# A hybrid streaming layer on one core: the sink column is written after the score product, VectorE makes every low half of a weight, and the second phase is laid out with another table of costs

## The chip, the cores and the metric

The kernel runs on one core of one Trainium2 chip. The metric is the device time of one execution in microseconds (us): 1554.15 us before the change, the median of three runs (1549.72 to 1560.18). Engines are named as the profile names them: PE is TensorE (PEld its weight load), DVE is VectorE, ACT is ScalarE, POOL is GpSimd, and SP is SyncE, which only issues transfers.

## The reference, cut to what matters

One layer of a streaming encoder, for 2048 prompt frames and 32 sample frames, 1024 wide, in fp32:

```python
h = rmsnorm(x, ln_g)
q, k, v, gate_a, b_gate, c_gate, u_in, gate_c, merge_a, merge_c = split(h @ w_in)
q, k = rope(rmsnorm(q)), rope(rmsnorm(k))             # 8 q heads, 2 kv heads, 64 wide
s = q @ k.T                                           # own chunk of 64 and the two before it
m = maximum(max(s), sink)
p = exp(s - m) / (sum(exp(s - m)) + exp(sink - m))    # sink: one learned number per head
y_a = (p @ v * silu(gate_a)) @ w_attn_out
y_c = (b_gate * conv3(c_gate * u_in) * silu(gate_c)) @ w_conv_out
r = x + (sigmoid(merge_a) * y_a + sigmoid(merge_c) * y_c) @ w_o
out = r + sigmoid(r @ w_ple_gate) * (p_in @ w_ple_proj)
```

The sink takes part in the softmax like one more key whose score is a constant.

## The kernel before

**Precision.** A product in fp32 is made of three products of split operands: each operand x is kept as a high half (a copy in the type fp32r) and a low half (x minus the high half), and hi·hi, hi·lo and lo·hi are added in PSUM. So every operand costs a copy on ACT (`..._h`) and a subtraction (`..._l`), and every 128x512 block of weights a cast on ACT and a subtraction, both written into a tile `w`.

**Two phases.** The first phase (to about 850 us) makes h @ w_in by a Strassen scheme and leaves its parts in DRAM. The second phase, the one the change touches, does everything else: yB (the convolution branch times its output weights), pp (p_in @ w_ple_proj), 17 attention tiles of 128 frames (16 of the prompt, with two chunks of 64 frames each, and one of the 32 sample frames), yA (attention times its weights), and two large products per half of the frames, UO (with w_o) and UPG (with w_ple_gate), again by a Strassen scheme; these are the `b` of the profile, and their results `c`. Their inputs `xb` are split too, after sums and differences on DVE (`tk`, `c`).

**Attention.** A chunk's chain, in `sink_attention` (L1230), is: ACT copies the sink into one column of the PSUM tile `S` (L1235); PE makes the scores into the columns beside it; DVE takes the negative maximum of scores and sink (`nm`, L1246); ACT makes the exponentials with their sum (`E`, L1253); DVE takes the reciprocal (`se`); ACT scales (`P`); PE transposes (`PT`); ACT and DVE split the result (`pth`, `ptl`); PE multiplies by the values (`O`); DVE multiplies by the gate (`at`). Since the copy of L1235 and the products write one tile, the product stands behind the copy. Ahead of the chain, a tile's queries and keys are transposed (`pq`, `pkv`), normed and rotated on DVE (`tt`, `ss`, `kn`, `qr`, `kr`) with two operations on POOL (`ab`, and a power of -0.5 on `ss`), transposed back (`pk`, `pqt`) and split (`KH`, `KL`, `qs`).

**What sets the order.** In the second phase no scheduler moves anything: a small planner inside the kernel, run while the program is built, writes each engine's instructions in the order in which its own clock reaches them. Each operation goes through `Engine` (L115), which asks `cost` (L101) for a duration, adds it to that engine's `busy` time and notes when the result is there; a step that needs a result is entered into a list with that time plus 0.15 (`SEM`). PE's clock `now` moves by PE's costs alone; `due` (L173) takes the next step whose time has come and whose buffers are free. So attention steps, evictions and splits are laid between PE's products according to these costs. The attention tiles are started at fixed amounts of PE's work, two chunks of a tile 5 us apart (`GAP`, L1992).

**Weights.** `split_w` (L1884) makes a block's halves: the cast on ACT and then the subtraction, on POOL for blocks ahead of `last_split` (L1895: the first block of the second half's large products), 88 of them, and on DVE for those after it. Five tiles `w` are in use at a time.

Since all of this goes through `Engine`, nearly every instruction of the second phase has line L136 in the profile, and the names of the tiles tell them apart.

Of the kernel before, what the change touches and what calls it, by code (L numbers as in the profile page):

```python
# [7 lines left out]
F32 = mybir.dt.float32  # L8
F32R = mybir.dt.float32r
AF = mybir.ActivationFunctionType  # L10
ALU = mybir.AluOpType
# [31 lines left out]
def tile_hybrid_stream_step(ctx: ExitStack, tc: tile.TileContext, x, xT, pT, wu, consts, rope, ckT, cv_dup,  # L43
                            ck_raw, cv_raw, yT, kpo, vpo, cpo, kso, vso, cso):
    nc = tc.nc
    add, sub, mul = ALU.add, ALU.subtract, ALU.mult
# [10 lines left out]
    def bank(name):  # L57
        return psp.tile([P, 512], F32, tag="ps", name=name)
# [28 lines left out]
    now, fin, seq, events = [0.0], [0.0], [0], []  # L87
    busy = {"V": 0.0, "S": 0.0, "G": 0.0, "Y": 0.0}
# [6 lines left out]
    def size(ap):  # L95
        n = 1
        for d in ap.shape[1:]:
            n *= d
        return n

    def cost(key, op, kw):  # L101
        if op == "dma_start":
            return 0.9 if kw.get("accum_op") is not None else 0.57 if key == "G" else 0.42
        n = size(kw["out"])
        if key == "T":
            return max(0.109, 0.00044 * n + 0.0064)
        if key == "S":
            return 0.2 + 0.00082 * n + (0.13 if kw.get("accum_out") is not None else 0.0)
        if key == "G":
            return 2.03 if kw.get("op") == ALU.pow else 0.35 + 0.0021 * n  # L110
        if op == "tensor_reduce":
            return 0.08 + 0.0012 * size(kw["in_"])
        return 0.3 if n <= 16 else 0.13 + 0.0011 * n

    class Engine:  # L115
        def __init__(self, key, engine):
# [2 lines left out]
        def __getattr__(self, op):  # L119
            f = getattr(self.engine, op)  # L120

            def call(**kw):
                us = cost(self.key, op, kw)
                if self.key == "T":
                    now[0] += us
                    end = now[0]
                else:
                    busy[self.key] = end = max(busy[self.key], now[0]) + us
                if op == "dma_start":
                    if wire[0] is None:  # L130
                        end += 6.6 if kw.get("accum_op") is not None else 5.2
                    else:
                        o = kw["out"]
                        wire[0] = end = max(end + 1.7, wire[0]) + o.shape[0] * size(o) * 4 / 390e3
                fin[0] = max(fin[0], end)
                return f(**kw)  # L136
            return call

    eV, eS, eG, eT, eY = [Engine(*x) for x in (("V", nc.vector), ("S", nc.scalar), ("G", nc.gpsimd), ("T", nc.tensor),
                                           ("Y", nc.sync))]  # L140
# [5 lines left out]
    def free(tag, n=1):  # L146
        live[tag] -= n
        assert live[tag] >= 0, tag
# [40 lines left out]
    def restart():  # L189
        assert not events  # L190
        now[0], banks[0], wire[0] = 0.0, 0, None
        for x in (busy, live):
            for k in x:
                x[k] = 0
        live["k"] = 24
# [25 lines left out]
    G = len(groups)  # L221
# [78 lines left out]
    def tile_of(gs, q):  # L300
        return "AB GF DE C".split().index(next(x for x in "AB GF DE C".split() if q in x)) if len(gs) == 2 else q == "C"

    worder = []
    for s in steps:
        for s_ in s:
            key = ("s", *s_) if len(s_) == 3 else ("l", *s_[1:3], tile_of(s_[1], s_[3]))
            if key not in worder:
                worder.append(key)
    for kind, b, n, *p in plan:
        key = {"B": (kind, b, n, *p), "yB": ("q", 0, UY + n, 1), "pp": ("pp", b, n // 2),  # L310
               "yA": ("q", b, UY + n, 0)}[kind]
        key = ("pp", 2, n // 2) if kind == "pp" else key
# [181 lines left out]
    def norm(v, k, rb, q):  # L494
        nc.vector.scalar_tensor_tensor(out=v, in0=v, scalar=lng_sb[:, k:k + 1], in1=rb[:, :q], op0=mul, op1=mul)
# [8 lines left out]
    B, T = {}, {}  # L504
# [718 lines left out]
    nc.gpsimd.memset(sq, EPS)  # L1223

    restart()
    order[0] = lambda e: e[:3]

    def sink_attention(name, ng, lhs, krhs, cn, e_out, norm, keys, sk, done, last, lag):  # L1230
        GG = 2 * ng
        SS = []
        for kv in range(2):
            s = bank(f"S_{name}_{kv}").rearrange("p (g c) -> p g c", g=2)
            eS.copy(out=s[:, :ng, cn:cn + 1], in_=sk[:, kv * ng:(kv + 1) * ng].unsqueeze(2))  # L1235
            kh, kl = krhs(kv)
            for j in range(ng):
                eT.matmul(out=s[:, j, :cn], lhsT=lhs(kv, j), rhs=kh, start=True, stop=False)
                eT.matmul(out=s[:, j, :cn], lhsT=lhs(kv, j), rhs=kl, start=False, stop=True)
            SS.append(s)  # L1240
        if last:
            free("qs")
        yield {}
        nmax = sm.tile([P, 4], F32, tag="nmax", name=f"nm_{name}")
        for kv in range(2):
            eV.tensor_reduce(out=nmax[:, kv * ng:(kv + 1) * ng], in_=SS[kv][:, :ng, :cn + 1],  # L1246
                            axis=AX.X, op=ALU.max, negate=True)
        yield {}
        se = sm.tile([P, 4], F32, tag="se", name=f"se_{name}")
        for kv in range(2):  # L1250
            for j in range(ng):
                g = kv * ng + j
                eS.activation(out=e_out(kv, j), in_=SS[kv][:, j, :cn + 1], func=AF.Exp, bias=nmax[:, g:g + 1],  # L1253
                              accum_out=se[:, g:g + 1])
            yield None
            yield None
        yield {}
        free("ps", 2)
        eV.reciprocal(out=se[:, :GG], in_=se[:, :GG])
        yield {}  # L1260
        for kv in range(2):
            for j in range(ng):
                g = kv * ng + j
                for src, dst in norm(kv, j):
                    eS.activation(out=dst, in_=src, func=AF.Copy, scale=se[:, g:g + 1])
            if kv == 0:
                yield None
        fin[0] += lag
        yield {"ps": 2, "ph": 1}
        w = ng * P  # L1270
        pts, parts = [], []
        for q0 in range(0, len(keys), 512 // w):
            qs = keys[q0:q0 + 512 // w]
            pp = bank(f"PT_{name}_{q0}")
            for i, (ins, kp_, vh, vl) in enumerate(qs):
                for j, src in enumerate(ins):
                    eT.transpose(out=pp[:kp_, i * w + j * P:i * w + (j + 1) * P], in_=src, identity=ident)
            cols = 256 if q0 else 512
            ph = sm.tile([P, cols], F32R, tag=f"pth{cols}", name=f"pth_{name}_{q0}", bufs=2)
            pl = sm.tile([P, cols], F32R, tag=f"ptl{cols}", name=f"ptl_{name}_{q0}", bufs=2)  # L1280
            i = 0
            while i < len(qs):
                e = i
                while e < len(qs) and qs[e][1] == qs[i][1]:
                    e += 1
                n = qs[i][1]
                parts.append((ph[:n, i * w:e * w], pl[:n, i * w:e * w], pp[:n, i * w:e * w]))
                i = e
            pts += [(ph[:n, i * w:(i + 1) * w], pl[:n, i * w:(i + 1) * w], vh[:n], vl[:n])
                    for i, (_, n, vh, vl) in enumerate(qs)]  # L1290
        yield {}
        free("P")
        for h, _, src in parts:
            eS.copy(out=h, in_=src)
        yield {}
        for x, (h, lo, src) in enumerate(parts):
            if x:
                yield None
            eV.tensor_tensor(out=lo, in0=src, in1=h.bitcast(F32), op=sub)
        yield {"ps": -1}  # L1300
        O = bank(f"O_{name}")
        for i, (ph, pl, vh, vl) in enumerate(pts):
            eT.matmul(out=O[:, :w], lhsT=vh, rhs=ph, start=(i == 0), stop=False)
            eT.matmul(out=O[:, :w], lhsT=vl, rhs=ph, start=False, stop=False)
            eT.matmul(out=O[:, :w], lhsT=vh, rhs=pl, start=False, stop=(i == len(pts) - 1))
        yield {}
        free("ph")
        done(O)
        yield {}
        free("ps")  # L1310
        if last:
            last()
# [571 lines left out]
    def split_w(i):  # L1884
        w = wp.tile([P, 2, 4, P], F32R, tag="w", name=f"w{i}")
        W2[i] = h, lo = w[:, 0], w[:, 1]
        src = raw_of.pop(i)
        eS.copy(out=h, in_=src)
        yield {}
        (eG if i < last_split else eV).tensor_tensor(out=lo, in0=src, in1=h.bitcast(F32), op=sub)  # L1890
        yield {}
        w_ready[i] = now[0]
        room["wf"] += 1

    last_split = next(i for i, key in enumerate(worder) if key[:2] == ("B", 1))  # L1895
    x_at, load_at = [0], [0]
    LEAD, LOOK = 2, 11

# [89 lines left out]
    T, t = {}, 0.0  # L1988
# [116 lines left out]
```

## Time and profile before

| what | value |
|---|---|
| median of three runs | 1554.15 us (1549.72 to 1560.18) |
| the profiled execution | 1554.51 us, its span 1552.7 us |
| mean granted clock of PE | 0.990 |
| busy, whole span: PE, DVE, ACT, POOL | 1504.6, 1219.8, 816.9, 491.6 us |
| 830 to 1086 us (A): PE, DVE, ACT, POOL | 241.69, 184.32, 156.63, 81.07 of 256 us |
| 1086 to 1330 us (B): PE, DVE, ACT, POOL | 221.83, 217.39, 159.71, 134.55 of 244 us |
| 1330 to 1540 us (C): PE, DVE, ACT, POOL | 210.00, 158.99, 96.56, 42.85 of 210 us |

The span runs from the first to the last instruction; the execution's own time is 1.8 us longer. A is the stretch of yB, pp, yA of the first quarter and about half of the attention; B holds the first half's large products and the rest of the attention; C is the second half's large products. A row of grouped instructions gives the count, the busy time and the mean duration of one, then the idle time of the engine ahead of them and what ended it. A row of waits gives who waited for whom, the total in us, the number of times and the longest. Engines work in order, and a duration in the profile includes the time in which an operation that has been started is held up.

### The profile page before, as it was taken

Reading aid. Unit: us, or ns where it says so; the run is one execution under the profiler, and the core shown is the slowest. Engines: PE = TensorE matmul, PEld = TensorE weight load, DVE = VectorE, ACT = ScalarE, POOL = GpSimd, SP = SyncE. Lnnn points to the kernel's source line nnn. Section 1 sums busy time; section 2 is a strip of 40 time slices with the busy share of each in tenths; the row PEclk is TensorE's granted clock in tenths of the full one; section 3 lists DMA queues with packets and bytes.
Section 4 is the critical chain, followed back from the end, with each engine's and each line's share of the span. In section 5 each row is a group of like instructions: output and inputs, shape, how many; then the busy total and the mean of one; then the engine's idle time right before and its main releaser. Section 6 shows DMA issues by size and latency. Waiting matters only on the chain. (4 is left out here: it accounts for less than half of the span.)

```text
span 1552.7 us, 28012 instructions
## 1 busy us (share of the span) xinstructions
PE 1504.6 (97%) x9553; PEld 1358.6 (87%) x9553; DVE 1219.8 (79%) x2242; ACT 816.9 (53%) x1933; POOL 491.6 (32%) x622
## 2 busy tenths in 40 slices
PE   9999999999999999999999999999988997999998
PEld 7878888888899999999999899887877886999998
DVE  7887878875689777899757678857799899569777
ACT  8453353344467544344556356775755676444453
POOL 2133322232212332344212222236647455410201
PEclk9999999999999999999999999999999999999999
DMA  9489886898778845344647766567847659995959
GB/s 336 156 295 341 312 301 211 270 348 274 248 255 276 284 160 159 118 135 133 196 162 251 246 221 202 185 184 222 195 122 197 155 170 270 256 266 143 256 146 279
DMA packets 199230, 346.88 MB, mean 223 GB/s; under 512 B 23728, under 2 KB 57072, under 8 KB 199088
## 3 DMA queue, kind: packets, MB, share of 16 engines
q1 hardware_dynamic: 157008, 239.42, 48.2%
q0 software_dynamic: 32432, 87.85, 19.8%
q10 hardware_dynamic: 9648, 17.83, 3.1%
q8 instruction: 75, 1.23, 0.3%
q14 instruction: 67, 0.55, 0.1%
HBM read 227.66 MB, written 117.46 MB: 222 GB/s over the span
## 5 line engine op out<-in xcount | busy, mean ns | idle before, releaser
L136 PE MATMUL b<-xb_h,w 128*128 128x264 f32 (+1 forms) x1344 | 314.2, 325 | 0.0
L136 PEld LDWEIGHTS b<-xb_h,w 128*128 128x128 f32 x1344 | 225.5, 190 | 19.0
L591 PE MATMUL a<-x_l,w 128*128 128x264 f32 (+1 forms) x744 | 228.1, 320 | 0.0
L589 PE MATMUL a<-x_h,w 128*128 128x264 f32 (+1 forms) x744 | 227.2, 320 | 0.1
L136 PE MATMUL b<-xb_l,w 128*128 128x264 f32 (+1 forms) x672 | 218.1, 325 | 0.0
L594 PE MATMUL a<-x_h,w 128*128 128x264 f32 (+1 forms) x744 | 201.5, 320 | 0.0
L207 ACT CAST w<-wr 128x512 fp32r<-128x512 f32 (+1 forms) x180 | 110.1, 618 | 105.2 <-PE c L594 34.5
L208 DVE TENSOR_TENSOR w<-wr,w 128x512 fp32r<-128x512 f32 (+1 forms) x180 | 136.6, 769 | 34.4 <-ACT w L207 34.0
L136 POOL TENSOR_TENSOR w<-wr,w 128x512 fp32r<-128x512 f32 x88 | 127.0, 1495 | 110.5 <-ACT w L136 96.1
L136 ACT CAST w<-wr 128x512 fp32r<-128x512 f32 x168 | 102.5, 620 | 106.1 <-PE b L136 31.5
L589 PEld LDWEIGHTS a<-x_h,w 128*128 128x128 f32 x744 | 139.9, 188 | 10.8 <-DVE s L795 0.3
L591 PEld LDWEIGHTS a<-x_l,w 128*128 128x128 f32 x744 | 139.7, 188 | 10.7
L136 PEld LDWEIGHTS b<-xb_l,w 128*128 128x128 f32 x672 | 127.8, 190 | 9.5
L594 PEld LDWEIGHTS a<-x_h,w 128*128 128x128 f32 x744 | 125.0, 188 | 10.5
L727 PE MATMUL la<-x_h,w 128*128 128x264 f32 x516 | 111.7, 285 | 1.2 <-ACT w L207 1.2
L589 PE MATMUL c<-x_h,w 128*128 128x512 f32 (+1 forms) x336 | 110.6, 340 | 0.0
L591 PE MATMUL c<-x_l,w 128*128 128x512 f32 (+1 forms) x336 | 110.7, 339 | 0.0
L207 ACT CAST w<-a 128x512 fp32r<-128x512 f32 x82 | 49.7, 621 | 98.2 <-DVE a L338 31.8
L594 PE MATMUL c<-x_h,w 128*128 128x512 f32 (+1 forms) x336 | 100.4, 340 | 0.0
L788 DVE SCALAR_TENSOR_TENSOR u<-u,c 128x264 f32<-128x264 f32 (+1 forms) x125 | 59.4, 507 | 44.8 <-ACT u L783 29.8
L136 PE MATMUL yB<-ycs_h,w 128*128 128x264 f32 (+1 forms) x384 | 91.0, 326 | 0.0
L136 PE MATMUL yA<-ac_h,w 128*128 128x264 f32 (+1 forms) x384 | 90.5, 325 | 0.0
(436 smaller groups left out, 3949.0 us busy)
## 6 DMA issues: line engine op xcount, KB each, us to landing
wr<-in_wu SPq DMA_DIRECT2D x177, 256.0 KB, 4.0
a<-in_wu SPq DMA_DIRECT2D x116, 256.0 KB, 5.2
wr<-ws SPq DMA_DIRECT2D x74, 256.0 KB, 3.5
wr<-qs SPq DMA_DIRECT2D x64, 256.0 KB, 4.1
ws<-a POOLq DMA_DIRECT2D x63, 256.0 KB, 4.0
qs<-a POOLq DMA_DIRECT2D x24, 256.0 KB, 5.7
z_s<-s2n POOLq DMA_DIRECT2D x21, 264.0 KB, 4.2
s<-z_s SPq DMA_DIRECT2D x21, 264.0 KB, 5.0
```

What stands on the lines that cost most here:

```text
L136: return f(**kw)
L207: nc.scalar.copy(out=hi, in_=src)
L208: nc.vector.tensor_tensor(out=lo, in0=src, in1=hi.bitcast(F32), op=sub)
L589: nc.tensor.matmul(out=ps[:, :cn], lhsT=w[:, 0, k], rhs=x[0][:, c0:c0 + cn], start=first and k == 0, stop=False, skip_group_check=True)
L591: nc.tensor.matmul(out=ps[:, :cn], lhsT=w[:, 0, k], rhs=x[1][:, c0:c0 + cn], start=False, stop=False, skip_group_check=True)
L594: nc.tensor.matmul(out=ps[:, :cn], lhsT=w[:, 1, k], rhs=x[0][:, c0:c0 + cn], start=False, stop=k == 3, skip_group_check=True)
L727: nc.tensor.matmul(out=ps[:, :m], lhsT=w[:, a, k], rhs=r[:, cols], start=q in "ABG" and j == 0 and e == 0, stop=j == 1 and e == 2, skip_gr ...
L788: nc.vector.scalar_tensor_tensor(out=t[:, c0:c0 + cn], in0=t[:, c0:c0 + cn], scalar=-1.0, in1=ps[:, :cn], op0=mul, op1=sub)
```

## The change

1. In `sink_attention`, the copy of the sink into its column comes after both products, as a step of its own; the maximum follows it as before.
2. In `split_w`, all subtractions go to DVE: the 88 that POOL made are now DVE's.
3. From the start of the second phase the planner uses a second table of costs, `cost_queue`. It charges an operation of DVE 0.085 less and one of ACT 0.1 less than `cost` did (a reduction 0.07 less, a very small operation on DVE 0.09 in place of 0.3), PE nearly the same, an accumulating transfer on POOL 0.6 in place of 0.9. The result is noted as there 0.08 (DVE), 0.1 (ACT) or 0.25 (POOL) after the engine is free (`LATE`), and each operation of POOL that isn't a transfer also charges DVE 0.35 of its cost (`BESIDE`).

The reads and writes, the amount of arithmetic, the transfers and their sizes are the same.

```diff
+    LATE = {"V": 0.0, "S": 0.0, "G": 0.0, "Y": 0.0}
+    BESIDE = [0.0]
+
     def cost(key, op, kw):
+        if LATE["V"]:
+            return cost_queue(key, op, kw)
         if op == "dma_start":
             return 0.9 if kw.get("accum_op") is not None else 0.57 if key == "G" else 0.42
         n = size(kw["out"])
...
+    def cost_queue(key, op, kw):
+        if op == "dma_start":
+            return 0.6 if key == "G" else 0.42
+        n = size(kw["out"])
+        if key == "T":
+            return max(0.1085, 0.000446 * n + 0.0028)
+        if key == "S":
+            return 0.1 + 0.00082 * n + (0.13 if kw.get("accum_out") is not None else 0.0)
+        if key == "G":
+            return 2.03 if kw.get("op") == ALU.pow else 0.35 + 0.0021 * n
+        if op == "tensor_reduce":
+            return 0.01 + 0.0012 * size(kw["in_"])
+        return 0.09 if n <= 16 else 0.045 + 0.0011 * n
+
     class Engine:
...
-                    busy[self.key] = end = max(busy[self.key], now[0]) + us
+                    busy[self.key] = max(busy[self.key], now[0]) + us
+                    end = busy[self.key] + LATE[self.key]
+                    if self.key == "G" and op != "dma_start":
+                        busy["V"] = max(busy["V"], now[0]) + BESIDE[0] * us
...
     restart()
+    LATE.update(V=0.08, S=0.1, G=0.25)
+    BESIDE[0] = 0.35
     order[0] = lambda e: e[:3]
...
             s = bank(f"S_{name}_{kv}").rearrange("p (g c) -> p g c", g=2)
-            eS.copy(out=s[:, :ng, cn:cn + 1], in_=sk[:, kv * ng:(kv + 1) * ng].unsqueeze(2))
...
         if last:
             free("qs")
+        yield {}
+        for kv in range(2):
+            eS.copy(out=SS[kv][:, :ng, cn:cn + 1], in_=sk[:, kv * ng:(kv + 1) * ng].unsqueeze(2))
         yield {}
         nmax = sm.tile([P, 4], F32, tag="nmax", name=f"nm_{name}")
...
-        (eG if i < last_split else eV).tensor_tensor(out=lo, in0=src, in1=h.bitcast(F32), op=sub)
+        eV.tensor_tensor(out=lo, in0=src, in1=h.bitcast(F32), op=sub)
```

The first phase's instructions stand as before. In the second, three places show what the change moves. The first is ACT around the sink copies of chunk 20 (`S_20_0`, `S_20_1`), in stretch B; `xb050_6_3_h` and its like are high halves of inputs of a large product, `c12_...` an eviction of one, `sq` and `VH` belong to the next attention tile. Before:

```order
L136 ACTIVATE sq_10098<-pkv2_3_13621 128x2x64
L136 CAST w396_13651<-wr396_13304 128x512
L136 CAST VH_10094<-pkv2_3_13621 64x64 x4
L136 COPY c12_050_3_1_13668<-b050_3_1_0_13603 128x512
L136 ACTIVATE xb050_6_3_h_13675<-tk0_3_12617 128x512
L136 ACTIVATE xb050_7_0_h_13683<-tk1_0_13005 128x512
L136 COPY S_20_0_13691<-cst_69 128x2
L136 COPY S_20_1_13697<-cst_69 128x2
```

and with the change:

```order
L158 ACTIVATE xb050_6_2_h_13594<-tk0_2_12635 128x512
L158 CAST w395_13606<-wr395_13270 128x512
L158 COPY c12_050_2_1_13623<-b050_2_1_0_13589 128x512
L158 COPY S_20_0_13629<-cst_69 128x2
L158 COPY S_20_1_13634<-cst_69 128x2
L158 CAST w396_13654<-wr396_13343 128x512
```

The copies now stand ahead of the next tile's `sq` and `VH` and of the weight block w396, which they stood behind; the product itself stands 24 matmuls earlier in PE's order than it did.

The second is DVE around the maxima of the same chunk (`nm_20`). Before:

```order
L136 TENSOR_TENSOR tt2_3_13636<-pkv2_3_13621,ab2_3_13624 128x256
L136 TENSOR_REDUCE ss2_3_13656<-sq_10098 128x10
L136 TENSOR_TENSOR c11_050_3_2_12917<-c11_050_3_2_12917,b050_3_1_0_13603 128x512
L136 SCALAR_TENSOR_TENSOR xb050_6_3_l_13676<-tk0_3_12617,xb050_6_3_h_13675 128x512
L136 SCALAR_TENSOR_TENSOR xb050_7_0_l_13684<-tk1_0_13005,xb050_7_0_h_13683 128x512
L136 TENSOR_REDUCE nm_20_13712<-S_20_0_13691 128x2
```

and with the change:

```order
L158 TENSOR_TENSOR w395_13606<-wr395_13270,w395_13606 128x512
L158 TENSOR_TENSOR tk1_7_13456<-tk1_7_13456,tc1_7_13458 128x512
L158 TENSOR_TENSOR c11_050_2_2_12899<-c11_050_2_2_12899,b050_2_1_0_13589 128x512
L158 TENSOR_TENSOR tk1_3_13382<-tk1_7_13456,tk1_3_13382 128x512
L158 SCALAR_TENSOR_TENSOR tk0_3_12693<-tk0_3_12693,tk1_3_13382 128x512
L158 TENSOR_REDUCE nm_20_13665<-S_20_0_13629 128x2
L158 TENSOR_REDUCE nm_20_13665<-S_20_1_13634 128x2
L158 TENSOR_TENSOR w396_13654<-wr396_13343,w396_13654 128x512
```

The subtractions of w395 and w396 stand in DVE's queue around the maxima, which come before the next tile's `tt` and `ss`.

The third is POOL near the end of the same product's evictions, in the middle of B (`c..<-in_xT` are accumulating transfers, `ss` is the power, `KH` and `KL` copies of keys). Before:

```order
L136 TENSOR_TENSOR ss3_0_14301<-ss3_0_14301,nhalf_70 128x10
L136 DMA c12_050_2_1_13626<-in_xT 128x512
L136 TENSOR_TENSOR w410_14357<-wr410_13934,w410_14357 128x512
L136 TENSOR_TENSOR w411_14359<-wr411_13992,w411_14359 128x512
L136 TENSOR_TENSOR w412_14383<-wr412_14091,w412_14383 128x512
L136 DMA c12_050_3_1_13668<-in_xT 128x512
L136 TENSOR_TENSOR w413_14415<-wr413_14109,w413_14415 128x512
L136 COPY KH_10092<-KH_10092 128x2x128
L136 COPY KL_10093<-KL_10093 128x2x128
```

and with the change:

```order
L158 TENSOR_TENSOR ss3_0_14356<-ss3_0_14356,nhalf_70 128x10
L158 DMA c12_050_2_1_13623<-in_xT 128x512
L158 DMA c12_050_3_1_13688<-in_xT 128x512
L158 DMA c21_050_0_7_13900<-in_xT 128x512
L158 DMA c21_050_1_7_13929<-in_xT 128x512
L158 COPY KH_10092<-KH_10092 128x2x128
L158 COPY KL_10093<-KL_10093 128x2x128
```

POOL keeps its transfers, powers and copies, and none of the four subtractions.

More of the change, by code (lines that the diff above doesn't have):

```diff
@@ L1893, in split_w @@
         room["wf"] += 1
-    last_split = next(i for i, key in enumerate(worder) if key[:2] == ("B", 1))
     x_at, load_at = [0], [0]
```

## The prediction

> **What bounds the kernel now.** I read the page's engine line first, then busy time by stretch, then PE's waits, then PE's clock, and last DVE's and POOL's groups in the stretch that loses most.
>
> ```profile
> PE 1504.6 (97%) x9553; PEld 1358.6 (87%) x9553; DVE 1219.8 (79%) x2242; ACT 816.9 (53%) x1933; POOL 491.6 (32%) x622
> ```
> ```profile
> core 0: us, PE busy (x) PEld busy (x) DVE busy (x) ACT busy (x) POOL busy (x), PEclk, DMA share, GB/s
> 830.00:1086.00 256.00, 241.69 (x1638) 221.78 (x1637) 184.32 (x389) 156.63 (x487) 81.07 (x72) 0.98 0.70 219
> 1086.00:1330.00 244.00, 221.83 (x1122) 184.49 (x1121) 217.39 (x357) 159.71 (x454) 134.55 (x113) 0.96 0.72 188
> 1330.00:1540.00 210.00, 210.00 (x1718) 209.53 (x1717) 158.99 (x299) 96.56 (x182) 42.85 (x47) 1.00 0.83 220
> ```
>
> PE bounds the whole, and no amount of PE's work is changed. So the change can only win what PE loses: idle time and lowered clock. In C (1330 to 1540) PE is never idle, and the 13 us after it are the last results' way out: nothing to win. A loses 14.3 us, B 22.2 us, and only these have a clock below 1. B is also where DVE is fullest, 217.4 of 244 us. PE's waits in A, then in B:
>
> ```profile
> PE S L136 <- ACT S L136: 5.1, 5, 2.5
> PE S L136 <- DVE kn L136: 3.8, 1, 3.8
> PE pq L136 <- DMA zq<-z_q: 3.0, 1, 3.0
> ```
> ```profile
> PE S L136 <- ACT S L136: 13.3, 6, 5.8
> PE O L136 <- DVE ptl L136: 8.7, 3, 5.1
> ```
>
> Nearly everything is a score product S that waits for the sink copy on ACT. (The wait put down to kn is one too: it is the 4.0 us in which ACT was busy 3.95, two rows below.) After such gaps the clock is halved. Of the windows here, 1007.9, 1076.4 and 1130.2 are gaps, the others the halved stretches behind these and behind two gaps at O:
>
> ```profile
> 1007.90:1011.90 4.00, 0.27 (x3) 0.06 (x1) 3.71 (x11) 3.95 (x16) 2.52 (x2) 1.00 0.94 271
> 1011.90:1015.30 3.40, 3.37 (x15) 3.37 (x16) 3.20 (x7) 0.88 (x4) 0.00 (x0) 0.50 0.16 48
> 1076.40:1079.20 2.80, 0.34 (x4) 0.13 (x2) 2.77 (x9) 2.80 (x11) 2.80 (x5) 1.00 0.74 233
> 1080.10:1083.50 3.40, 3.40 (x14) 3.01 (x14) 1.31 (x4) 1.29 (x3) 0.81 (x2) 0.51 0.66 205
> 1134.80:1141.60 6.80, 5.14 (x16) 4.47 (x17) 5.39 (x11) 5.07 (x14) 4.51 (x4) 0.50 0.46 93
> 1203.00:1209.80 6.80, 6.03 (x18) 5.06 (x19) 6.73 (x13) 2.77 (x8) 2.46 (x2) 0.50 0.56 148
> 1319.10:1325.90 6.80, 6.09 (x22) 5.51 (x23) 3.79 (x9) 4.01 (x14) 3.02 (x3) 0.50 0.96 233
> ```
>
> Half of the busy time in these is lost: 1.7 + 1.7 = 3.4 us in A, 2.6 + 3.0 + 3.0 = 8.6 us in B. So a gap of 3 us costs nearly 5.
>
> Why is ACT late with its copies in B? Because it waits for DVE, and DVE for POOL:
>
> ```profile
> 1308.54 5.78 DVE L136 SCALAR_TENSOR_TENSOR ac_l<-acf,ac_h 128x528 fp32r<-128x528 f32 x1
> ```
> ```profile
> 1308.42 5.32 POOL L136 TENSOR_TENSOR w<-wr,w 128x512 fp32r<-128x512 f32 x4
> ```
>
> One DVE operation takes 5.78 us, exactly as long as four subtractions of weights on POOL run. It isn't one accident. The groups of DVE in B, and the two after them in the stretch 1340 to 1540, where POOL has almost no such work:
>
> ```profile
> L136 DVE TENSOR_TENSOR xb_l<-c,xb_h 128x512 fp32r<-128x512 f32 x28 | 29.1, 1054 | 2.4 <-ACT xb_h L136 2.2
> L136 DVE TENSOR_TENSOR c<-c,b 128x512 f32<-128x512 f32 x35 | 23.6, 677 | 7.1 <-PE b L136 5.6 <-ACT c L136 1.4
> L136 DVE SCALAR_TENSOR_TENSOR xb_l<-tk,xb_h 128x512 fp32r<-128x512 f32 x20 | 18.4, 940 | 0.1
> L136 DVE SCALAR_TENSOR_TENSOR c<-c,c 128x512 f32<-128x512 f32 x12 | 12.5, 1045 | 0.1
> L136 DVE SCALAR_TENSOR_TENSOR c<-c,pp 128x512 f32<-128x512 f32 x13 | 11.0, 853 | 0.1
> L136 DVE SCALAR_TENSOR_TENSOR ac_l<-acf,ac_h 128x528 fp32r<-128x528 f32 x4 | 7.9, 1970 | 0.0
> L136 DVE TENSOR_TENSOR kn<-tt 128x64 f32<-128x64 f32 x12 | 6.9, 572 | 0.0
> L136 DVE TENSOR_TENSOR VL<-pkv,VH 64x64 fp32r<-64x64 f32 x24 | 5.3, 220 | 0.3
> ```
> ```profile
> L136 DVE TENSOR_TENSOR w<-wr,w 128x512 fp32r<-128x512 f32 x64 | 43.7, 686 | 9.7 <-ACT w L136 9.3 <-DMA pp<-z_pp 0.2
> L136 DVE TENSOR_TENSOR xb_l<-c,xb_h 128x528 fp32r<-128x528 f32 x28 | 19.0, 701 | 1.8 <-ACT xb_h L136 1.7
> ```
>
> Operations that read PSUM (c<-c,b, VL) keep 677 and 220 ns; those that read two tensors from SBUF are held up. Over 680 ns (701 for ac_l, 220 for kn) that is 28 x 0.374 + 20 x 0.26 + 12 x 0.365 + 13 x 0.173 + 4 x 1.27 + 12 x 0.352 = 31.6 us in B. The smaller groups add some more.
>
> **The change part by part.** *The sink copy behind the product.* It takes away the waits at S: 5.1 + 3.8 = 8.9 us in A, 13.3 us in B. The copy itself stays on ACT and now lies in the chain between product and maximum:
>
> ```profile
> 1078.91 0.28 ACT L136 COPY S<-cst 128x2 f32<-128x2 f32 x2
> ```
>
> So each of the 32 prompt chunks' chains becomes at least 0.28 us longer, and where ACT's queue is late the maximum is late. That costs nothing as long as PE has other products between S and PT, as it has: PE never waits at PT in A or B, and ACT waits for PE there instead:
>
> ```profile
> ACT pth L136 <- PE PT L136: 15.7, 6, 8.7
> ```
>
> If that cover were gone, the price would be 32 x 0.28 = 9 us or more. The copy can now hold up ACT until PE has made the product; queued behind it at chunk 20 is the cast of w396, then DVE's half of w396. Late next after S are PT (on P) and O (on ptl).
>
> *The subtractions.* POOL loses and DVE gains 25 in A, 58 in B and 5 after it:
>
> ```profile
> L136 POOL TENSOR_TENSOR w<-wr,w 128x512 fp32r<-128x512 f32 x58 | 84.3, 1524 | 55.0 <-ACT w L136 52.4 <-DMA pp<-z_pp 1.6 <-issue 0.7
> L136 POOL TENSOR_TENSOR ss<-ss,nhalf 128x10 f32<-128x10 f32 x6 | 13.0, 2169 | 6.6 <-DVE ss L136 6.6
> L136 POOL TENSOR_TENSOR ab<-cs,cst 128x256 f32<-128x256 f32 x6 | 6.6, 1094 | 0.0
> ```
> ```profile
> L136 POOL TENSOR_TENSOR w<-wr,w 128x512 fp32r<-128x512 f32 x25 | 34.7, 1405 | 55.3 <-ACT w L136 43.5 <-ACT S L136 11.8
> ```
>
> A duration of 0.68 isn't what one takes of DVE's time, since starts are closer:
>
> ```profile
> 1126.42 0.68 DVE L136 TENSOR_TENSOR tk<-tk,tc 128x512 f32<-128x512 f32 x1
> 1127.02 0.67 DVE L136 TENSOR_TENSOR c<-c,b 128x512 f32<-128x512 f32 x1
> ```
>
> 0.60 us from start to start. So DVE gains 58 x 0.60 = 34.8 us in B. What it gets back is the hold-up by these 58: they are 84.3 of the 103.9 us of POOL's arithmetic above, 81%, so 0.81 x 31.6 = 25.6 us. DVE in B: 217.4 - 25.6 + 34.8 = 226.6 us. In A: 184.3 + 25 x 0.60 = 199.3 of 256 us, well covered by PE. So in B DVE isn't relieved; its work is even a little more. What changes is its kind: lumps of 2 to 6 us that the planner knew nothing of become operations of 0.6 us that stand in its table. And the floor of B is no longer PE's 221.8 less its 8.6 of half clock, 213 us, but DVE's 227, if DVE were never idle.
>
> *The order.* Costs nothing by itself. It takes 0.085 to 0.1 us per operation out of the plan, which was a margin by accident (0.69 planned against 0.60 from start to start) and is now given to the 88 subtractions and to POOL's hold-ups.
>
> **The sum**, against the profiled execution's 1554.5 us (0.4 above the median, so no correction). A: 8.9 us of waits and 3.4 of clock go; the wait for zq (3.0 us, a transfer) stays; with longer chains and less margin I take 3 back at PT and O: gain 9.3. B: between 227 us (DVE never idle) and 244 (nothing gained). DVE now idles 26.6 us in B, mostly waiting for PE's own products (5.6 in the row of c<-c,b), and these come sooner when PE doesn't wait. I take the end near the full DVE, 231: gain 13. C: 0. 1554.5 - 9.3 - 13 = 1532 us.
>
> On the clock, the Trainium skill's "TensorE: Matmul & The Clock Gate" (What's actually happening) says that PE falls to half its clock after at least one idle window of about 3.4 us. By that the gap of 2.8 us at 1076.4 wouldn't have led to the half clock behind it, and A's gain would be 1.7 less, 1534 us in all; the trace shows the half clock, so I keep it.
>
> **Rivals.**
> *DVE isn't the floor (PE runs through).* Weights and inputs of the large products are prepared far ahead, so DVE's backlog may run over into C, where it is busy 159 of 210 us. Then B falls to 213 and A gives all: 1554.5 - 12.3 - 31 = 1511 us. For it: no wait of PE for w or xb in the rows. Against: attention's DVE operations stand in the same queue. Chance 0.12.
> *The waits move (no change).* S no longer waits, but PT and O do: ACT's and DVE's backlog is still there, the plan lost its margin and each chain got the copy. An ACT chain of ten operations from S to P loses 10 x 0.1, gets back two handovers of 0.1 and pays the copy's 0.28: about 1 us per chunk. If 25 of 33 chunks stall by it: 1532 + 25 = 1557 us. For it: the O waits, already there at 8.7. Against: none at PT. Chance 0.14.
> *DVE saturates (slower).* If the hold-up doesn't go with POOL's subtractions (the powers and transfers that remain hold DVE as long), DVE in B needs 217.4 + 34.8 = 252 us, and with the 26.6 idle it has now 279: 35 more, 1554.5 - 9.3 + 35 = 1580 us. It decides as soon as less than 8 us of the 31.6 go, with DVE never idle. Against: the 5.78 us beside four POOL subtractions, and 686 ns per w where POOL is quiet. Chance 0.07.
> *DVE holds POOL.* The 58 subtractions on DVE read two tensors from SBUF and may hold POOL's powers just as POOL's held DVE: 7 in B by up to 0.68, 5 us in the chain ss, kr, pk; 1537 us. Chance 0.05. The Trainium skill's "SBUF — State Buffer" (SBUF: two separate sides) says so: whichever of the two starts first has the shared ports for its whole instruction, and the other is blocked; the 5.78 us agree for POOL first, no row here shows the other way alone.
>
> **How the numbers follow.** The forecast, B near DVE's floor, has 0.62; its own range is 1518 to 1544, from no give-back in A and B at 220 (the smaller held-up groups counted too) to B at 240 and a gain of 6 in A. The range of 8 in 10 reaches to the first two rivals: 1511 to 1553. A measurement of this kernel can tell about 1% from no change, 15.5 us. Faster by more (below 1539): 0.62 x 0.9 + 0.12 + 0.05 x 0.6 = 0.71, and some of the moved waits: 0.74. Slower by more: 0.07, and 0.02 of the moved waits: 0.09. Within 1%: 0.17.
>
> **What would show it.** Right: no row of PE at S waiting for ACT; POOL's w gone, DVE's w x88 more; xb_l<-c back near 700 ns in B; DVE's busy time in B at 215 to 230 of a shorter stretch; PE's remaining waits at O and PT below 10 us; C unchanged; fewer half-clock stretches, with the one behind zq left. Wrong: xb_l still near 1 us; PE waiting at PT or O for 20 us; PE waiting for w or xb.

## The result and the profile after

The changed kernel takes 1530.11 us (median of four runs, 1526.45 to 1533.35); the kernel before took 1552.41 us on the same chip (median of four, 1549.72 to 1560.18). The ratio is 0.9848, with a 95% interval of 0.9804 to 0.9892, all of it below 1: faster, by about 22 us or 1.5%. The profiled execution took 1533.35 us, its span 1531.6.

The page's engine line, and the busy time by stretch; A, B and C now end at 1076, 1312 and 1525 us:

```profile
PE 1500.7 (98%) x9553; PEld 1355.8 (89%) x9553; DVE 1227.2 (80%) x2330; ACT 818.2 (53%) x1933; POOL 370.5 (24%) x534
```
```profile
830.00:1076.00 246.00, 239.72 (x1654) 221.44 (x1653) 191.66 (x416) 159.50 (x493) 48.20 (x47) 0.99 0.72 226
1076.00:1312.00 236.00, 222.82 (x1141) 184.94 (x1140) 216.84 (x419) 159.88 (x443) 55.52 (x57) 0.96 0.74 199
1312.00:1525.00 213.00, 213.00 (x1752) 213.00 (x1751) 165.71 (x310) 98.25 (x192) 34.55 (x40) 1.00 0.83 228
```

PE's losses in A shrink from 14.3 to 6.3 us and in B from 22.2 to 13.2 us; C has none, as before. DVE makes 62 operations more in B than before and is busy for as long, 216.84 us against 217.39. POOL is busy for 55.5 us there in place of 134.6. PE's waits in A and then in B:

```profile
PE pq L158 <- DMA zq<-z_q: 3.2, 1, 3.2
PE lc L749 <- DVE o L765: 1.3, 1, 1.3
PE pp L158 <- ACT E L158: 1.0, 1, 1.0
PE PT L158 <- ACT P L158: 0.7, 1, 0.7
```
```profile
PE b L158 <- DVE c L158: 4.5, 3, 3.3
PE PT_s L158 <- ACT Ps L158: 3.2, 1, 3.2
PE b L158 <- ACT xb_h L158: 2.8, 1, 2.8
PE pq L158 <- ACT E L158: 1.4, 1, 1.4
PE b L158 <- DVE xb_l L158: 0.8, 2, 0.5
PE PT L158 <- ACT P L158: 0.5, 1, 0.5
```

No score product waits for a copy, and no O for ptl. The copy waits for the product now, which costs ACT time that it has; in B:

```profile
ACT S L158 <- PE S L158: 14.3, 17, 5.2
```

What is left in B are a few waits of the large products: for an eviction that frees a bank (c), for inputs (xb), and one for the sample frames' scaled exponentials (Ps). Three of these waits (for xb_h, Ps and c) and the one for zq each end in a halved clock. In the windows over these four places, the window and its length come first, then the busy time of PE, PEld, DVE, ACT and POOL, and the clock is the third figure from the right:

```profile
883.50:886.90 3.40, 3.40 (x18) 3.38 (x17) 0.17 (x1) 1.43 (x4) 0.73 (x1) 0.50 1.04 397
1125.80:1129.20 3.40, 3.40 (x13) 2.92 (x13) 2.93 (x9) 3.40 (x12) 0.17 (x1) 0.51 0.54 77
1207.80:1214.60 6.80, 5.63 (x17) 4.68 (x18) 6.62 (x17) 3.41 (x11) 1.98 (x1) 0.50 0.25 69
1272.60:1279.40 6.80, 5.63 (x13) 4.46 (x14) 6.80 (x13) 1.83 (x3) 0.47 (x1) 0.50 1.07 315
```

DVE's groups in B that were held up before:

```profile
L158 DVE TENSOR_TENSOR w<-wr,w 128x512 fp32r<-128x512 f32 x60 | 43.2, 723 | 0.5 <-ACT w L158 0.2
...
L158 DVE TENSOR_TENSOR xb_l<-c,xb_h 128x512 fp32r<-128x512 f32 x28 | 18.6, 682 | 3.0 <-ACT xb_h L158 2.9
...
L158 DVE SCALAR_TENSOR_TENSOR xb_l<-tk,xb_h 128x512 fp32r<-128x512 f32 x20 | 13.8, 715 | 0.6 <-ACT xb_h L158 0.5
L158 DVE SCALAR_TENSOR_TENSOR c<-c,pp 128x512 f32<-128x512 f32 x15 | 10.2, 684 | 0.1
...
L158 DVE SCALAR_TENSOR_TENSOR c<-c,c 128x512 f32<-128x512 f32 x12 | 8.1, 685 | 0.2
...
L158 DVE SCALAR_TENSOR_TENSOR ac_l<-acf,ac_h 128x528 fp32r<-128x528 f32 x4 | 2.6, 696 | 0.0
```

Operations that took 853 to 1970 ns take 682 to 715. The 60 new ones in B have 43.2 us of busy time, and at the prediction's 0.60 us from start to start they take 36 of DVE's. Since DVE's total in B stands, the hold-up that went is about as large (an estimate from these rows). So DVE got 60 operations more in B and no more load there; in the whole execution it is busy for 1227.2 us in place of 1219.8.

### The profile page after: what moved, and what is told of

The parts are those of the page before. It is cut to its first block, busy times and chain, and to the rows that moved or that the text cites. A ratio compares the mean times of both kernels' runs of the same rounds, so it can differ in the third digit from the quotient of the medians.

```text
span 1531.6 us, 27944 instructions
## 1 busy us (share of the span) xinstructions
PE 1500.7 (98%) x9553; PEld 1355.8 (89%) x9553; DVE 1227.2 (80%) x2330; ACT 818.2 (53%) x1933; POOL 370.5 (24%) x534
## 4 chain that ended last, share of the span: by engine, by line
PE 38%; DVE 7%; ACT 3%; DMA 2%; issue 2%; SPq 0%; ACTq 0%; DVEq 0%
PE b L158 17%; PE yB L158 5%; PE yA L158 5%; PE O L158 2%; PE S L158 2%; DVE c L158 1%; PE la L749 1%; PE pp L158 1%; PE a L611 1%; PE a L613 1%; PE a L616 1%; PE PT L158 1%; DVE w L158 1%; DVE xb_l L158 1%; DVE tk L158 1%
## 5 line engine op out<-in xcount | busy, mean ns | idle before, releaser
L158 PE MATMUL b<-xb_l,w 128*128 128x264 f32 (+1 forms) x672 | 218.4, 325 | 0.8 <-DVE xb_l L158 0.8
L158 DVE TENSOR_TENSOR w<-wr,w 128x512 fp32r<-128x512 f32 x168 | 117.8, 706 | 14.1 <-ACT w L158 13.4
L805 ACT COPY u<-a 128x264 f32<-128x264 f32 (+1 forms) x114 | 47.4, 437 | 80.7 <-PE a L616 80.7
```

Of the source, the lines that this page charges most:

```text
L805: nc.scalar.copy(out=t[:, c0:c0 + cn], in_=ps[:, :cn])
```

## The experiments

The change has three edits, so the first question is which of them carries the gain: each alone, and the change without each. Then the hold-up is measured by itself, then the parts of the table. All stretches below are cut at the same products of PE (the starts of the 5,001st, the 6,652nd and the last of the 9,540 in its order, without the first 13 of the execution's 9,553), from the trace's start times: A is then 257.8 us before and 245.9 after. The order moves attention across the border of B and C, so these two are taken together: 460.3 before, 449.0 after; where they are told apart below, the border is the 7,788th product. The stretches are those of one execution of each kernel, the medians those of several. How far a stretch can be trusted shows in the kernel of "The load of queries" below, which is nearly the changed one: 249.9 and 444.3 us.

| sink copy behind | subtractions on DVE | new table | median, us | ratio to before (95%) | A | B and C |
|---|---|---|---|---|---|---|
| | | | 1552.41 | 1 | 257.8 | 460.3 |
| x | | | 1549.68 | 0.9977 (0.9962 to 0.9991) | 247.4 | 466.6 |
| | x | | 1568.77 | 1.0095 (1.0073 to 1.0117) | 267.0 | 464.2 |
| | | x | 1566.09 | 1.0083 (1.006 to 1.0107) | 260.7 | 470.2 |
| x | x | | 1548.9 | 0.997 (0.9954 to 0.9986) | 248.1 | 463.1 |
| | x | x | 1546.87 | 0.9942 (0.9925 to 0.9959) | 257.3 | 457.4 |
| x | | x | 1537.13 | 0.9884 (0.9869 to 0.9899) | 245.8 | 455.9 |
| x | x | x | 1530.11 | 0.9848 (0.9804 to 0.9892) | 245.9 | 449.0 |

Each ratio is to the kernel before as it ran beside that kernel (medians of 1552.41 to 1555.11). The kernels ran on several chips, so ratios are compared before medians.

### The sink copy alone

```diff
-            eS.copy(out=s[:, :ng, cn:cn + 1], ...)          # ahead of the products
+        yield {}                                            # behind them
+        for kv in range(2):
+            eS.copy(out=SS[kv][:, :ng, cn:cn + 1], ...)
```

> Only the sink copy is moved behind the product; POOL keeps its 88 subtractions and the planner its first table. Theory 1 (two causes: the product waited for ACT's copy, and POOL's subtractions held DVE up; the table only arranges): the waits at S go, 8.9 us in A and 13.3 in B, but DVE is still held up in B and the lateness shows at O and PT, so about half of B's comes back: 1552 - 9 - 5 = 1538 us, xb_l<-c still near 1050 ns. Theory 2 (the table of costs makes the gain): within 5 us of 1552. Theory 3 (the hold-up hurts only through the sink copy, so this edit alone is the whole gain): 1530 us.

1549.68 us, 0.9977. A does what was expected of it, 10.4 us less. B and C take 6.3 us more. PE's waits in B:

```profile
PE b L136 <- DVE c L136: 4.5, 3, 4.0
PE b L136 <- DVE xb_l L136: 4.4, 2, 3.4
PE pk L136 <- DVE kr L136: 4.3, 1, 4.3
PE b L136 <- ACT w L136: 4.0, 1, 4.0
PE S L136 <- DVE qs L136: 3.2, 1, 3.2
PE b L136 <- ACT xb_h L136: 3.1, 2, 2.2
PE b L136 <- ACT c L136: 1.6, 1, 1.6
```

Not one is at S for the copy, and together they are 25.1 us, where PE lost 22.2 before. xb_l<-c still takes 961 ns. In B, it seems, the copy was only the first place at which a late DVE and ACT were noticed. The time is theory 2's (within 5 us of 1552), though its reason leaves A's gain out. Theory 1 had A's gain, but expected half of B's to come back, and all of it did. Theory 3 is out.

### The subtractions alone

```diff
-        (eG if i < last_split else eV).tensor_tensor(out=lo, in0=src, in1=h.bitcast(F32), op=sub)
+        eV.tensor_tensor(out=lo, in0=src, in1=h.bitcast(F32), op=sub)
```

> Only the subtractions go to DVE; the sink copy stays ahead of its product and the planner keeps its first table. Theory 1: the hold-up in B goes (xb_l<-c near 690 ns) and with it the late copies there, A keeps its waits at S, 5 to 9 us: 1552 - 10 = 1542 us. Theory 2: 1552 us or slower. Theory 3: a copy that is late because ACT's own queue is full stays late, 1548 us.

1568.77 us, slower than before by 0.95%: theory 2's "1552 us or slower", against the 1542 and 1548 of the others. The hold-up does go (B's groups), but PE waits for w (PE's waits in B), and A has its waits at S and more (PE's waits in A):

```profile
L136 DVE TENSOR_TENSOR xb_l<-c,xb_h 128x512 fp32r<-128x512 f32 x28 | 19.9, 725 | 0.9 <-ACT xb_h L136 0.7
```
```profile
PE b L136 <- DVE w L136: 9.1, 3, 4.2
PE b L136 <- ACT xb_h L136: 4.6, 2, 4.2
```
```profile
PE S L136 <- ACT S L136: 12.1, 6, 3.2
PE PT L136 <- ACT P L136: 4.0, 1, 4.0
```

The larger part of the loss lies in A, 9.2 us, and B and C take 3.9 us more. The order has moved too. Chunk 31's score product is the 7,742nd of PE's products before, the 7,872nd here: the planner has put attention some 130 products later. C, which waits for that attention's result (yA for ac_h, 3.2 us), takes 222.6 us in place of 213.5, and B 241.7 in place of 246.7.

### The table alone, and the change without the table

```diff
     restart()
+    LATE.update(V=0.08, S=0.1, G=0.25)
+    BESIDE[0] = 0.35
```

> Only the planner's table is changed (with the sink copy ahead and POOL subtracting, both charged as the new table has it). Theory 1: same or a little slower, 1545 to 1560 us, with S waiting as before or more, since the plan has less margin. Theory 2: 1533 us.

1566.09 us, slower by 0.83%, against theory 2's 1533 and above theory 1's 1545 to 1560: the new table on the old kernel wins nothing. PE waits for the copy 16 times, where it did 11 times:

```profile
PE S L158 <- ACT S L158: 19.7, 16, 3.2
PE pk L158 <- DVE kr L158: 6.1, 4, 2.8
```

The change without these two lines:

> The change without its new table: sink copy moved, all subtractions on DVE, planned with the first table. Theory 1: most of the gain is here, 1530 to 1538 us. Theory 2: 1548 us or more.

1548.9 us. So theory 1's "the table only arranges" falls: by the ratios (0.997 against 0.9848) four fifths of the gain, some 19 us, are there only with the table. Theory 2 (the table makes the gain) has this number but missed the one above. A is near the changed kernel's, 248.1; B and C, 463.1, are not, and the last chunk's product stands at the 7,872nd place again. PE's waits in B:

```profile
PE b L158 <- DVE xb_l L158: 7.1, 3, 4.3
PE b L158 <- DVE c L158: 5.1, 2, 3.9
PE b L158 <- DVE w L158: 3.8, 2, 2.0
```

All three are for DVE. The new theory: with the subtractions on it, DVE has 419 operations in B, and the first table charges most of them 0.085 us more than the second, 36 us in all. If the second is what they take, the plan holds some 217 + 36 = 253 us of DVE in a stretch of 236 and defers what doesn't fit. Before the change the same excess was 357 x 0.085 = 30 us on 186 us (217.4 less the hold-up of 31.6), 216 us in 244, and fitted. These sums are estimates from the counts and busy times of the traces; the plan itself was not printed.

### The change without the sink edit, and without the subtractions

```diff
-        yield {}
-        for kv in range(2):
-            eS.copy(out=SS[kv][:, :ng, cn:cn + 1], ...)
+            eS.copy(out=s[:, :ng, cn:cn + 1], ...)          # ahead of the products
```

> The change with the sink copy ahead of its product again; subtractions on DVE, new table. After the first four runs: the copy is worth 10 us in A (sink_alone) and in B its waits move elsewhere. Theory 1, revised (three edits that need each other): A at 256 us, B at 240, 1530 + 14 = 1544 us. If subtractions and table carry the gain by themselves: 1532 us.

1546.87 us, near the 1544 of theory 1 in its revised form. A is 257.3, B and C 457.4. PE's waits in the whole:

```profile
PE S L158 <- ACT S L158: 16.5, 12, 2.9
```

The copy alone was worth 0.2%, and in company of the other two some 15 us, or 0.9% (against 1532.0 us, next but one section, beside it on the same chip).

```diff
-        eV.tensor_tensor(out=lo, in0=src, in1=h.bitcast(F32), op=sub)
+        (eG if i < last_split else eV).tensor_tensor(out=lo, in0=src, in1=h.bitcast(F32), op=sub)
```

> The change with the 88 subtractions on POOL again; sink copy moved, new table. Theory 1, revised: A like the changed kernel's, 247 us; in B the hold-up is back (xb_l<-c near 1000 ns), 246 to 250 us: 1530 + 12 = 1542 us. If gains simply add up (cost_alone 1566, sink_alone 5 us below before): 1561 us. If the hold-up costs nothing once the product waits for no copy: 1531 us.

1537.13 us: between what the hold-up was expected to cost and nothing, and 5 us above the 1532.0 beside it. A is the changed kernel's, B and C take 6.9 us more. DVE is held up again (B's groups), and O waits (PE's waits in B):

```profile
L158 DVE TENSOR_TENSOR xb_l<-c,xb_h 128x512 fp32r<-128x512 f32 x28 | 25.6, 927 | 0.4 <-ACT xb_h L158 0.3
```
```profile
PE O L158 <- DVE ptl L158: 7.0, 2, 3.5
```

So gains don't add up, and the subtractions' move is the smallest of the three where the other two are made.

### The hold-up by itself

The changed kernel, with its order on every engine but POOL, and 88 subtractions of the same size on POOL whose operands and result are one tile that nothing else in the second phase uses:

```diff
+        if i < last_split:
+            nc.gpsimd.tensor_tensor(out=idle_t[:, :4], in0=idle_t[:, :4], in1=idle_t[:, :4], op=sub)
         eV.tensor_tensor(out=lo, in0=src, in1=h.bitcast(F32), op=sub)
...
+    idle_t = const.tile([P, 5, P], F32, tag="dg", name="idle_t", bufs=1)
```

> The changed kernel, instruction for instruction on PE, DVE, ACT and SP, with 88 subtractions of the same size added on POOL that read and write a tile of their own, so that nothing waits for their result. If POOL's reading of SBUF holds DVE up: xb_l<-c back near 1000 ns and w on DVE too, about 30 us more of DVE in B, which has none to spare: 1530 + 20 = 1550 us or more. If the cost of POOL's subtractions was that their result came late: 1530 us, durations unchanged.

1572.72 us, 1.0113 (1.0098 to 1.0129), some 41 us above the kernel with the earlier load of queries (1532.0 us, next section), which ran beside it on the same chip. B by the windows, and groups of DVE and POOL in it:

```profile
1084.00:1351.00 267.00, 229.99 (x1133) 188.65 (x1133) 255.92 (x416) 158.54 (x442) 126.28 (x115) 0.93 0.68 175
```
```profile
L158 DVE TENSOR_TENSOR w<-wr,w 128x512 fp32r<-128x512 f32 x60 | 55.0, 921 | 0.3
L158 DVE TENSOR_TENSOR c<-c,b 128x512 f32<-128x512 f32 x35 | 23.8, 679 | 3.2 <-PE b L158 2.1 <-ACT c L158 0.8
L158 DVE TENSOR_TENSOR xb_l<-c,xb_h 128x512 fp32r<-128x512 f32 x28 | 22.5, 819 | 2.4 <-ACT xb_h L158 2.3
...
L1917 POOL TENSOR_TENSOR idle_t<-idle_t 128x512 f32<-128x512 f32 x59 | 79.0, 1340 | 2.1
```

Nothing waits for these 88 results, and DVE is busy for 255.9 us in B in place of 216.8, for 416 operations in place of 419. B is 267 us long, 31 more. So what POOL's subtractions cost DVE is not a late result. The price is larger than expected: DVE, at 92% already, passes 31 of the 39 us on to PE.

### The load of queries

```diff
-        t = 11 * e if e < 8 else ...
+        t = 11 * e - 4 * (e == 1) if e < 8 else ...
```

> The changed kernel with the second attention tile begun 4 us of PE's work earlier, so that its load of queries is issued earlier. The wait of PE for zq (3.2 us) and the half clock behind it (1.7 us) go if the load follows the start: 1530 - 5 = 1525 us. If the load is issued late because SP's queue stands at an earlier transfer: 1530 us.

1532.0 us, 0.9851 (0.9836 to 0.9865): no gain, but not for the reason expected, a load that SP issues late. In the trace the load is issued 3.1 us earlier (874.6 in place of 877.8) and lands after up to 6.1 us in place of 5.4, with all transfer engines busy (a share of 1.06 from 876 to 884 us); PE waits 4.4 us for it. PE's products stand in nearly the same order as in the changed kernel, so this run also confirms that kernel's time.

### The parts of the table

First: the first table, with only DVE's charges lowered to the new ones.

```diff
+    PITCH = [False]
...
-            return 0.08 + 0.0012 * size(kw["in_"])
-        return 0.3 if n <= 16 else 0.13 + 0.0011 * n
+            return (0.01 if PITCH[0] else 0.08) + 0.0012 * size(kw["in_"])
+        if PITCH[0]:
+            return 0.09 if n <= 16 else 0.045 + 0.0011 * n
...
-    LATE.update(V=0.08, S=0.1, G=0.25)
-    BESIDE[0] = 0.35
+    PITCH[0] = True
```

> Sink copy moved and subtractions on DVE, planned with the first table, in which only DVE's costs are lowered to the new table's (0.085 less per operation, a reduction 0.07 less). Theory: the first table books DVE beyond what it can hold in B once the 58 subtractions are there, so that the plan pushes attention back, into C (218.4 us without the new table, 213.3 with it). If DVE's cost per operation is what matters: B at 236 to 239 and C at 214 us, 1533 us. If it is the hand-over times or POOL's charge on DVE: like the kernel without the new table, 1549 us.

1530.11 us, 0.9857 (0.9832 to 0.9882): the whole effect of the table. Chunk 31's product is back at the 7,741st place; B and C take 446.8 us. So it is what DVE's operations are charged, and nothing else of the table, that the change needs. Where the time went without it shows in B by the windows, first of the change without the table, then of this run:

```profile
1076.00:1321.00 245.00, 226.23 (x1138) 187.88 (x1139) 214.27 (x411) 152.29 (x414) 56.72 (x58) 0.96 0.74 193
1073.80:1300.00 226.20, 216.41 (x1139) 179.88 (x1138) 214.09 (x417) 158.61 (x446) 56.67 (x57) 1.00 0.75 199
```

The difference is in B, 19 us: about half is PE's idle time (18.8 us against 9.8), the rest the lower clock. DVE's work is the same and DVE stood idle for 30.7 us there, so it was late rather than full. And C is no shorter with the new charges, 220.9 us against 218.4. So attention put off into C isn't where the time went. The two other parts, taken out of the changed kernel:

```diff
-    BESIDE[0] = 0.35
+    BESIDE[0] = 0.0
```

> The changed kernel with no charge on DVE for POOL's operations in the plan. DVE's hold-up by POOL is only some 6 us in the whole second phase of the changed kernel. If the charge is a mere margin: 1530 us, within 4. If the plan needs it: 1540 us or more, waits for ptl and qs.

1531.54 us, 0.9865 (0.9836 to 0.9894). The profiled execution is the longest of the four, 1537.73 us.

```diff
-    LATE.update(V=0.08, S=0.1, G=0.25)
+    LATE.update(V=0.000001, S=0.0, G=0.0)
```

> The changed kernel planned without the hand-over times of 0.08, 0.1 and 0.25 us behind each operation (the engines' costs as in the new table). If these are the margin that keeps PT and O from waiting: waits at PT, O and pk of 10 us or more, 1540 us. If DVE's and ACT's costs are enough: 1530 us, within 4.

1530.95 us, 0.9862 (0.9837 to 0.9886). Neither can be told from the changed kernel, though chunk 31's product stands at the 7,807th place in the second, 65 later than before the change. Last, a table that is finer still:

```diff
-            return 0.1 + 0.00082 * n + (0.13 if kw.get("accum_out") is not None else 0.0)
+            return (0.1 + 0.00082 * n + (0.13 if kw.get("accum_out") is not None else 0.0) + (0.06 if kw["out"].shape[0] == 64 else 0.0)
+                    + (0.0 if isinstance(kw.get("scale", 1.0), float) else 0.09))
...
-        return 0.09 if n <= 16 else 0.045 + 0.0011 * n
+        return 0.09 if n <= 16 else 0.045 + 0.0011 * n + (0.09 if kw["out"].shape[0] == 64 else 0.0)
...
-    BESIDE[0] = 0.35
+    BESIDE[0] = 0.12
```

> The changed kernel with a table nearer to the starts that the trace shows: 0.09 more for DVE's and 0.06 more for ACT's operations on 64 partitions, which start only 0.22 us apart for 64 columns, 0.09 more for ACT's scaling by a column, and 0.12 in place of 0.35 for POOL's charge on DVE. If the remaining waits in B come from costs that the table has wrong: B at 230 us, 1525 us. If they come from DVE being full: 1530 us.

1526.32 us, 0.9834 (0.9808 to 0.986): the lowest median of all, near the 1525 expected if the waits left in B come from the table. All its four executions (1524.75 to 1528.65) lie below all of the three kernels beside it (from 1528.67), but the intervals of the ratios overlap, so a gain of some 4 us is likely and not settled.

## Why the prediction was right, and where its reasons were not

**The time.** 1532 us was forecast, 1530 measured, and the sum's two terms came out close: A 9.3 forecast, 11.9 measured (257.8 to 245.9); B 13 forecast, 11.3 with C. That they add up to the measured gain of 22 us is in part luck: one was too small, the other too large, and most of the gain needs the edit that was put at nothing. The waits at S went, no wait at O came in their place, those at PT are 0.7, 0.5 and 3.2 us, and C stayed. Gone with them is the longest gap at S, which the prediction names without its row:

```profile
1130.20:1136.40 6.20, 0.42 (x2) 0.00 (x0) 5.30 (x8) 2.52 (x9) 1.80 (x1) 0.87 0.84 244
```

**The clock behind a gap.** "So a gap of 3 us costs nearly 5" holds for some gaps. PE's wait of 2.8 us for xb_h, until 1124.4 us, was followed by 3.4 us at a clock of 0.51 in the changed kernel, as the prediction had it for the gap at 1076.4. But the wait of 3.3 us for c, with 6.8 us at 0.50 in the changed kernel (from 1272.6), stands in the run with the earlier load too, from 1270.0 us, and no lowered clock goes with it there.

**A.** Right in mechanism: every kernel with the copy ahead has an A of 257 us or more, and the four of the table with the copy behind have 245.8 to 248.1. (With the copy behind, A was longer in two other profiles: 253.7 without POOL's charge on DVE, in that kernel's longest execution, and 256.1 with POOL kept busy.) The give-back of 3 us was too large; what came in A is 1.0 at pp and 0.7 at PT.

**DVE's floor in B.** The mis-sized term. 226.6 us of DVE were forecast, 216.8 measured: the hold-up that went was more than 0.81 x 31.6, since nearly all held-up groups are back near 690 ns, and the smaller ones too. (The 5.78 us of the one operation aren't "exactly as long" as the four subtractions of 5.32 beside it, but outlast them by 0.46.) So DVE wasn't the floor at 227, and B, at 236, is longer than the 231 that were taken. It is 13.2 us of PE's own waits that remain there, for evictions, inputs and one late Ps. That they come from places in the order and not from the amount of work is likely, since B takes 226.2 us for 214.1 of DVE's with the first table and DVE's new charges, but no run takes them away one by one.

**The order.** The step that failed is "Costs nothing by itself", with the table as a mere loss of margin. The change without the table is at 1549 us and the table alone at 1566. The forecast counted the first two edits as the whole gain; by themselves they gain 0.3%. What it overlooked may stand in its own numbers: 0.69 us planned against 0.60 from start to start is a margin as long as DVE has room, and with 58 operations more it books DVE beyond B's length. That lowering DVE's charges alone gives the whole effect is shown, and so is where the time goes without it: to PE's waits for DVE in B and the lower clock behind them. How the overbooked plan brings these about stays open. Attention put off into C, which the places in the order suggest, doesn't explain it: C is as long with the new charges, and the kernel without hand-over times has its last chunk at the 7,807th place at no loss.

**The rivals.** "The waits move" is what the sink copy does alone: 22 us at S and O become 25 us at seven other kinds of waits in B. In the whole change it doesn't happen. "DVE saturates" was put down to a hold-up that stays; the hold-up went, and the subtractions alone were slower all the same, 9.2 of their 13 us in A, with waits at S and PT; with the new table beside them A is back at 257.3. The run with POOL kept busy shows that its price was not too high: 255.9 us of DVE make a B of 267. "DVE holds POOL": POOL's power took 2169 ns before in B and 2104 after, among 60 more DVE operations that read two tensors from SBUF; no sign of it. "PE runs through" had B at 213; B took 236, with 13.2 us of PE's waits, and these aren't DVE's backlog alone.

## What to carry to other kernels

In a planner, try charging each operation the distance from start to start in the trace and not its duration: here an excess that was a margin while DVE's own work filled 186 of 244 us cost the change most of its gain once DVE was given more, and the edit that gave it more looked bad by itself. Where edits touch one order, try them together and take out one at a time; alone, two of the three here were slower and the third won a seventh of the whole. And look at what an engine's helper does to it: the work taken over by POOL cost DVE as much time in B as doing it (217.4 against 216.8 us).

## What the runs showed of the hardware that wasn't expected

88 subtractions on POOL, on a tile that DVE doesn't touch in the second phase, lengthened DVE's busy time in B, where 59 of them ran, by 39 us (216.8 to 255.9), and the kernel by about 41 us: nearly half a microsecond of the kernel's time for each of the 88. The Trainium skill's "SBUF — State Buffer" (SBUF: two separate sides) has VectorE and GpSimd share a pair of SBUF ports as an exclusive lock, for VectorE's operations with two SBUF inputs. The trace agrees: with POOL busy, operations of B that read PSUM kept their times (c<-c,b 681 ns in the changed kernel, 679 here), and those with two inputs from SBUF went from 682 to 819 ns (xb_l<-c) and from 723 to 921 ns (w).
